# Strassen's scheme moved from the MLPs' first product to their second

## The chip, the cores and the metric

The kernel runs on one core of one Trainium2 chip. A core has five engines with a queue each, in order: TensorE (PE in the profile; its weight loads are PEld), VectorE (DVE), ScalarE (ACT), GpSimd (POOL) and SyncE (SP, which issues the DMAs here). TensorE writes its sums into PSUM, eight banks of 128 x 512 float32; everything else lives in SBUF. The metric is the device time of one execution in microseconds, the median of several runs.

## The reference

A decoder trunk of two layers over 512 tokens of width 1024, in float32. Layer 0 mixes by two kinds of sparse attention, layer 1 by differential attention; each layer adds its mixer's output projection to the residual stream h and then the MLP, and a last norm follows.

```python
def sq_relu_mlp(h, w_up, w_down):
    u = jnp.einsum('btd,df->btf', h, w_up)
    return jnp.einsum('btf,fd->btd', jnp.square(jax.nn.relu(u)), w_down)

x = x + mixer(rms_norm(x, mix_norm_g[i]))
x = x + sq_relu_mlp(rms_norm(x, mlp_norm_g[i]), w_up[i], w_down[i])
```

`w_up` is 1024 x 4096, `w_down` 4096 x 1024, per layer.

## The kernel before

**Precision.** Every float32 product is made from three matmuls (`mm3`, L607): an operand is split into a high part, a copy rounded to the type `F32R`, made on ACT, and a low part, the rest, made by a subtraction on VectorE. high x high, high x low and low x high are added up in PSUM. A weight tile of 128 x 1024 therefore costs a DMA, a cast (L501) and a subtraction (L278, the helper `sub`, or L504).

**Order of the work.** The program is written as Python generators that a planner (`Sched`) runs while the kernel is built: each `op` names its engine, an estimated cost and a priority (a smaller number goes first), and the planner lays down each engine's instructions in the order that its model gives. On the chip each engine then runs its queue in that order. Where the planner sees TensorE idle, it lays down filler matmuls of zeros (L372, `junk`) that keep its clock up. Buffers are `Slots`: PSUM banks, 12 tiles `x4s` of SBUF, two raw weight tiles, weight tiles in pairs (high, low), two pairs outside the MLPs and four within (`Weights.run`, L449). Weights are loaded, cast and subtracted in the order of `plan` (L563), ahead of use as far as the slots reach; the first `w_up` loads of each layer are an exception, spawned at the start and waiting for the MLP's pool alone (`load_up`, L480).

**MLP** (`mlp`, L853). The 4096 hidden columns go in four groups of 1024; each group makes its part of u and adds its part of u² `w_down` to h. The first product uses the Strassen-Winograd scheme, seven products of half-sized blocks for eight: a group has two blocks of 512 hidden columns, and each block takes seven products (`product`, L874) of 24 matmuls of 256 columns, each product in half a pair of blocks. The four sums of the weights are made on VectorE (`split_up`, L514, tiles `ws`), the four sums of x once per layer (`Mixed.quarter`, L740, tiles `ts` and `xm`), and the products are put together on VectorE in SBUF (`sums`, L921: seven adds of 512 columns per block). The squared ReLU follows in `finish` (L910). The second product is plain (`gemm_tok`, L774, tag `down`): two halves of 512 output columns, 96 matmuls of 512 columns each, then `residual` (L808) adds the four banks to h and multiplies by the square of the norm's factor r, so that x needs no r before.

**Around it.** `out_proj` (L1983) runs in two passes over four column blocks; as each block of the second pass is added to h, a `quarter` of the MLP's x is made from it. At the end of layer 0, `follow` (L834) makes the eight chunks of layer 1's x (`Norm.chunk`, L629: four transposes on TensorE, a scaled copy on ACT, a subtraction on VectorE), the first four after the left half of h is whole, the last four after the right one. `odd` (L1773), layer 1's mixer, is started by `trunk` (L2094) when `block` of layer 0 has returned. It makes `qk` and `v` of four pairs of heads by `gemm_tok`, and one pass of `qk` holds four PSUM banks until it is evacuated with the factor r. `finish` (L2063) is the last norm: per row tile, POOL multiplies the left half of h by the gains once its sum of squares is there, then ACT scales the left and VectorE the right half.

Of the kernel before, what the change touches and what calls it, by code (L numbers as in the profile page):

```python
# [19 lines left out]
NT, ND = 4, 8  # L20
# [245 lines left out]
def trunk_kernel(ctx, tc, x, mix_g, mlp_g, w_in0, pe, cw1, cw2, w_out0, w_in1, lam, sub_g, w_out1,  # L266
# [148 lines left out]
    class Weights:  # L415


        def __init__(self):
            self.specs, self.ready = [], {}
            self.raw, self.w = Slots(sch, range(2)), Slots(sch, range(4))  # L420
            self.braw, self.st, self.pool = Slots(sch, range(2)), Slots(sch, range(3)), None
# [10 lines left out]
        def up(self, W, f0, layer):  # L432
            self.add("up", [W[k * 512:k * 512 + 512, f0:f0 + 512].rearrange("(k p) n -> p k n", p=128)
                            for k in range(2)], [128, 4, 512], layer)
# [4 lines left out]
        def move(self, a, b, n):  # L439

            for _ in range(n):
                i = yield a.get(prio=9)
                if i < 4:
                    b.put(i)
# [4 lines left out]
        def run(self):  # L449
            w, phase = self.w, None  # L450
            for i, spec in enumerate(self.specs):
                if spec[0] == "up" and self.specs[i - 1][3] is None:
                    spawn(self.load_up(i, None))
            for i, (tag, srcs, shape, layer, ready) in enumerate(self.specs):
                if layer != phase:
                    if layer is None:
                        spawn(self.move(w, self.w, 4 + 4))
                        w = self.w
                    else:
                        w = yield ev("wp", layer)  # L460
                        spawn(self.move(self.w, w, 4))
                    phase, n = layer, 0
                size = shape[1] * shape[2]
                if tag == "up":
                    n += 1
                    if n > 1:
                        spawn(self.load_up(i, w))
                    yield ready
                    continue
                r = yield self.raw.get()  # L470
                raw = wpool.tile(shape, F32, name="wraw", tag=f"wraw{r}")
# [5 lines left out]
                spawn(self.split(i, shape, raw, r, self.load(i, size, load), w, w.get(2), ready,  # L477
                                 i > 0 and layer is None))

        def load_up(self, i, w):  # L480
            tag, srcs, shape, layer, ready = self.specs[i]
            first = w is None
            if first:
                self.pool = yield ev("mp", layer)
                w = Slots(sch, range(4, 4 + 4))
                sch.set(ev("wp", layer), w)
            ids, futs = [w.get(2) for _ in UP], {m: Fut() for m in UP}
            rs, raws, fs = [], [], []
            for src in srcs:
                rs.append((yield self.braw.get()))  # L490
                raws.append(self.pool.tile(shape, F32, name="braw", tag=f"br{rs[-1]}"))
                fs.append(self.load(i, shape[1] * shape[2], lambda r=raws[-1], src=src: nc.sync.dma_start(r, src)))
            spawn(self.split_up(futs, raws, rs, fs, w, ids, None if first else False))
            sch.set(ready, futs)
# [14 lines left out]
        def split(self, i, shape, raw, r, loaded, w, ids, ready, both):  # L509
            yield loaded  # L510
            yield from self.halves(raw, shape, ids, w, ready, both)
            self.raw.put(r)

        def split_up(self, futs, raws, rs, loaded, w, ids, both):  # L514

            shape = [128, 4, 256]
            ids = dict(zip(UP, ids))
            (a11, a21), (a12, a22) = [[r[:, :, i * 256:i * 256 + 256] for i in range(2)] for r in raws]

            def part(m, src):  # L520
                return spawn(self.halves(src, shape, ids[m], w, futs[m], both))

            def total(x, y, o):
                k = yield self.st.get()
                s = self.pool.tile(shape, F32, name="ws", tag=f"ws{k}")
                yield sub(s, x, y, 1024, 1, o, both is None)
                return k, s

            yield loaded[0]
            f11 = part("a11", a11)  # L530
            yield loaded[1]
            f12 = part("a12", a12)
            k1, s1 = yield from total(a21, a22, OP.add)
            k2, s2 = yield from total(s1, a11, OP.subtract)
            f2 = part("s2", s2)
            k3, s3 = yield from total(a11, a21, OP.subtract)
            f3, f1 = part("s3", s3), part("s1", s1)

            def release(fs, slots, k):
                yield fs  # L540
                slots.put(k)

            spawn(release([f11], self.braw, rs[0]))
            spawn(release([f3], self.st, k3))
            spawn(release([f1], self.st, k1))
            k4, s4 = yield from total(a12, s2, OP.subtract)
            f4, f22 = part("s4", s4), part("a22", a22)
            spawn(release([f2], self.st, k2))
            spawn(release([f12, f22], self.braw, rs[1]))
# [1603 lines left out]
```

## Time and profile before

| | us |
|---|---|
| median of 3 runs (1280.49 to 1281.98) | 1281.44 |
| the profiled execution | 1279.79 |
| its span, first to last instruction | 1278.0 |
| VectorE busy | 919.4 |
| TensorE filler (L372, 266 matmuls) | 34.1 |
| mixer and projection of layer 0, to the first product of its MLP | 321.6 |
| MLP of layer 0, to its last matmul | 662.2 |
| mixer and projection of layer 1, to the first product of its MLP | 905.4 |
| MLP of layer 1, to its last matmul | 1268.6 |

A matmul's duration in the profile overlaps the next one's, so rates are read from starts. The filler counts as busy time of TensorE. A group's row ends with the idle time of the engine before these instructions and what ended it.

### The profile page before, as it was taken

How to read it: one execution, taken by the hardware profiler on the slowest of the kernel's cores; microseconds unless marked ns; L12 is line 12 of the kernel's file. 1: busy time of each engine (PE TensorE's matmuls, PEld its weight loads, DVE VectorE, ACT ScalarE, POOL GpSimd, SP SyncE). 2: the span in 40 equal slices, each digit the busy share in tenths (PEclk: the TensorE clock that was granted, in tenths of full speed). 3: DMA queues.
4: the chain of work that ended last, by engine and by line, in shares of the span. 5: the costliest groups of instructions: out<-in, count | busy, mean ns of one | idle time of the engine just before them, and what ended most of it. 6: DMA issues, size and time to landing. Idle time of an engine off the chain costs nothing.

```text
span 1278.0 us, 21371 instructions
## 1 busy us (share of the span) xinstructions
PE 1260.2 (99%) x8595; PEld 1114.1 (87%) x8595; DVE 919.4 (72%) x1466; ACT 577.0 (45%) x1149; POOL 269.4 (21%) x335
## 2 busy tenths in 40 slices
PE   9999999999999999999999999999999999999998
PEld 7998776779998989989888888889898898998987
DVE  4689986667975965948745687777697586594873
ACT  5556565554642422414334565564454242241332
POOL 1475785443100000000002335333110000000001
PEclk9999999999999999999999999999999999999999
DMA  6212422003232242231322222240423215223131
GB/s 191 73 45 76 116 85 66 18 17 109 91 112 87 80 151 95 75 129 67 115 89 96 65 67 67 66 133 30 153 67 99 100 67 165 80 86 132 67 99 66
DMA packets 78787, 114.70 MB, mean 90 GB/s; under 512 B 4288, under 2 KB 43616, under 8 KB 78688
## 3 DMA queue, kind: packets, MB, share of 16 engines
q1 hardware_dynamic: 78512, 113.27, 27.7%
q8 instruction: 67, 1.10, 0.4%
q14 instruction: 32, 0.26, 0.1%
q10 hardware_dynamic: 176, 0.07, 0.0%
HBM read 109.13 MB, written 4.19 MB: 89 GB/s over the span
## 4 chain that ended last, share of the span: by engine, by line
PE 86%; DVE 7%; ACT 2%; DMA 2%; issue 1%; POOL 1%; SPq 0%; POOLq 0%; DVEq 0%; ACTq 0%
PE b L608 24%; PE b L610 23%; PE b L609 23%; PE b L1076 4%; PE b L1615 2%; PE b L1602 2%; DMA braw<-in_mlp_w_up_dram 2%; PE b L1081 1%; PE b L372 1%; PE b L1037 1%; DVE ts L279 1%; PE b L1413 1%; DVE xm L279 1%; PE b L1900 1%; DVE ws L278 1%
## 5 line engine op out<-in xcount | busy, mean ns | idle before, releaser
L609 PE MATMUL b<-xm,w 128*128 128x256 f32 x896 | 253.9, 283 | 1.3 <-DVE xm L279 1.3
L610 PE MATMUL b<-xm,w 128*128 128x256 f32 x896 | 253.9, 283 | 0.8 <-DVE w L278 0.8
L608 PE MATMUL b<-xm,w 128*128 128x256 f32 x896 | 254.1, 284 | 0.3 <-ACT xm L716 0.3
L608 PE MATMUL b<-w,x 128*128 128x256 f32 (+3 forms) x768 | 243.7, 317 | 0.2 <-ACT eo L1860 0.2
L501 ACT CAST w<-wraw 128x1024 fp32r<-128x1024 f32 (+3 forms) x136 | 137.3, 1010 | 218.7 <-PE b L610 169.3
L609 PE MATMUL b<-w,x 128*128 128x256 f32 (+3 forms) x768 | 234.5, 305 | 0.3 <-DVE w L504 0.3
L610 PE MATMUL b<-w,x 128*128 128x256 f32 (+3 forms) x768 | 234.1, 305 | 0.0
L608 PE MATMUL b<-w,u 128*128 128x512 f32 x512 | 199.4, 389 | 0.0
L609 PE MATMUL b<-w,u 128*128 128x512 f32 x512 | 199.3, 389 | 0.0
L610 PE MATMUL b<-w,u 128*128 128x512 f32 x512 | 199.2, 389 | 0.0
L609 PEld LDWEIGHTS b<-xm,w 128*128 128x128 f32 x896 | 172.0, 192 | 2.1 <-DVE xm L279 1.7
L610 PEld LDWEIGHTS b<-xm,w 128*128 128x128 f32 x896 | 172.0, 192 | 1.4 <-DVE w L278 1.4
L608 PEld LDWEIGHTS b<-xm,w 128*128 128x128 f32 x896 | 172.0, 192 | 1.1 <-ACT xm L716 0.8
L608 PEld LDWEIGHTS b<-w,x 128*128 128x128 f32 x768 | 146.6, 191 | 10.1 <-issue 3.5
L609 PEld LDWEIGHTS b<-w,x 128*128 128x128 f32 x768 | 146.8, 191 | 5.8 <-DVE w L504 0.5
L610 PEld LDWEIGHTS b<-w,x 128*128 128x128 f32 x768 | 146.4, 191 | 5.7
L278 DVE TENSOR_TENSOR w<-wraw,w 128x1024 fp32r<-128x1024 f32 (+1 forms) x65 | 80.1, 1232 | 64.0 <-ACT w L501 64.0
L1021 POOL TENSOR_TENSOR raw<-raw,tm 128x512 f32<-128x512 f32 (+1 forms) x26 | 36.4, 1404 | 403.2 <-DVE raw L1018 381.5
L501 ACT CAST w<-ws 128x1024 fp32r<-128x1024 f32 x64 | 66.4, 1049 | 119.3 <-PE b L610 57.6
L610 PEld LDWEIGHTS b<-w,u 128*128 128x128 f32 x512 | 96.1, 188 | 20.0
L608 PEld LDWEIGHTS b<-w,u 128*128 128x128 f32 x512 | 96.1, 188 | 19.8
L609 PEld LDWEIGHTS b<-w,u 128*128 128x128 f32 x512 | 96.1, 188 | 19.6
(250 smaller groups left out, 2074.9 us busy)
## 6 DMA issues: line engine op xcount, KB each, us to landing
braw<-in_mlp_w_up_dram SPq DMA_DIRECT2D x32, 1024.0 KB, 6.7
wraw<-in_mlp_w_down_dram SPq DMA_DIRECT2D x64, 512.0 KB, 3.9
wraw<-in_odd_w_in_dram SPq DMA_DIRECT2D x32, 256.0 KB, 3.0
wraw<-in_even_w_in_dram SPq DMA_DIRECT2D x12, 512.0 KB, 3.7
wraw<-in_even_cmp_w_dram SPq DMA_DIRECT2D x16, 256.0 KB, 3.8
wraw<-in_even_w_out_dram SPq DMA_DIRECT2D x8, 512.0 KB, 4.4
wraw<-in_odd_w_in_dram SPq DMA_DIRECT2D x8, 512.0 KB, 3.5
q<-in_x_dram SPq DMA_DIRECT2D x4, 512.0 KB, 6.9
```

What stands on the lines that cost most here:

```text
L278: return op("dve", cv(n), lambda: nc.vector.tensor_tensor(o, x, y, op=alu), prio=prio, port=True)
L279: return op(DP, (cv(n), cg(n)), lambda e: e.tensor_tensor(o, x, y, op=alu), prio=prio, bias=0)
L372: nc.tensor.matmul(still[i][:, :256], z[:, :128], z[:, :256], start=True, stop=True)
L501: yield op("act", cas(size), lambda: nc.scalar.copy(wh, src), prio=1)
L608: nc.tensor.matmul(o, ah, bh, start=start, stop=False)
L609: nc.tensor.matmul(o, ah, bl, start=False, stop=False)
L610: nc.tensor.matmul(o, al, bh, start=False, stop=stop)
L1021: yield op("pool", cg(n), lambda: nc.gpsimd.tensor_tensor(o, v, t2, op=OP.add), prio=4)
L1037: nc.tensor.transpose(ps[:, tsl(j)], src, ident)
L1076: nc.tensor.matmul(s[:, j, :n], qs[j][a][half], k[h][b][half, :n], start=i + j == 0, stop=mask is None and i == 2)
L1602: nc.tensor.transpose(ps[:, tsl(k)], p_(a)[:, tsl(kb)], ident)
L1615: nc.tensor.matmul(po.columns(half)[64 * b:64 * b + 64], v1, pt[:, 256 * b:256 * b + 256], start=first, stop=last)
```

## The change

The first product becomes plain: per group four strips (`up`) of 256 hidden columns, each 48 matmuls of 512 columns in two banks, over an x that is kept whole in the MLP's pool (`Kept` in the place of `Mixed`). The factor r is now applied with the ReLU in `hidden`, from a tile `rows` that holds r along the free dimension in all partitions; `spread` makes it with a matmul of ones and a diagonal of r.

The second product takes the scheme, with tokens and output columns halved: u's forms (`a11`, `a12`, `s1` to `s4`, `a22`) are made per strip in `hidden`, the forms of `w_down` (`b11`, `b21`, `t1` to `t4`, `b22`) in `quarters`. Its seven products of 24 wide matmuls are accumulated in banks that are not cleared in between, and each bank's state is added to a quarter of h (`add`) when it stands for one. All 4096 hidden columns' weights are loaded once, as before, in 512 KB tiles; there are eight raw tiles within an MLP, and `w_up` has no path of its own in `Weights.run`.

The `odd` mixer is started at once; its products begin as soon as the chunks they read are there, and only their evacuation waits for the end of layer 0. They take the right half of x first (`ODD_ORDER`).

```diff
+    DOWN = ("b11", "b21", "t2", "t1", "t3", "b22", "t4")
+    ODD_ORDER = (2, 3, 0, 1)
...
+        def quarters(self, j, loaded, futs, ids, w, raws):
+            shape = [128, 2, 512]
...
+            b11 = yield from fetch("b11")
+            f11 = part("b11", b11)
+            b21 = yield from fetch("b21")
+            f21 = part("b21", b21)
+            b12 = yield from fetch("b12")
+            yield f11
+            yield sub(b11, b12, b11, 1024, 1)
+            b22 = yield from fetch("b22")
+            k = yield self.st.get()
+            t2 = self.pool.tile(shape, F32, name="ws", tag=f"ws{k}")
+            yield sub(t2, b22, b11, 1024, 1)
+            f2 = part("t2", t2)
+            spawn(release(part("t1", b11), "b11"))
+            yield sub(b12, b22, b12, 1024, 1)
+            spawn(release(part("t3", b12), "b12"))
+            spawn(release(part("b22", b22), "b22"))
+            yield f21
+            yield sub(b21, b21, t2, 1024, 1)
+            spawn(release(part("t4", b21), "b21"))
+            yield f2
+            self.st.put(k)
...
+        def spread(self):
+            yield ev(self.name, "r", 0, NT)
+            def a():
+                for t in range(NT):
+                    nc.vector.tensor_scalar(self.diag[:, tsl(t)], ident, self.r[:, t:t + 1], None, op0=OP.mult)
+            yield op("dve", 4 * cv(64), a, prio=1, port=True)
+            b = yield banks.get(prio=1)
+            ps = bank(b)
+            yield op("pe", 0.87, lambda: nc.tensor.matmul(ps, ones.bitcast(F32), self.diag, start=True, stop=True), prio=1)
+            yield op("act", ca(T), lambda: nc.scalar.copy(self.rows, ps), prio=1)
...
+            def prio(m, i):
+                k = ("a11", "a12", "s2", "s1", "s3", "s4", "a22").index(m)
+                return 2 if i >= 2 and k >= LATE else k - 9
+            def parts(g, i, m, src):
+                hi, lo = yield from form(g, m)
+                yield op("act", cas(256), lambda: nc.scalar.copy(hi[:, i], src), prio=prio(m, i))
+                yield sub(lo[:, i], src, hi[:, i].bitcast(F32), 256, prio(m, i))
+            def hidden(g, i, ids, ps):
...
+                def out(n):
+                    yield op("dve", cv(T) + 0.06, lambda: nc.vector.scalar_tensor_tensor(
+                        v[:, n], ps[n], 0.0, norm.rows, op0=OP.max, op1=OP.mult), prio=-1)
+                    banks.put(ids[n])
+                    yield op("act", cas(T), lambda: nc.scalar.activation(v[:, n], v[:, n], AF.Square), prio=-1)
...
+            def up(g, i):
+                ids = yield banks.get(2, prio=-1)
...
+                            for n in range(2):
+                                mm3(ps[n], wh[:, c, tsl(n)], wl[:, c, tsl(n)], norm.x(0, 4 * kb + c),
+                                    norm.x(1, 4 * kb + c), kb == 0 and c == 0, kb == 1 and c == 3)
+                        yield op("pe", 6 * cm(512), run, prio=9)
...
+                spawn(hidden(g, i, ids, ps))
+            def add(g, j, l, ps, last):
+                def one(n):
+                    t = 2 * j + n
+                    hs = h["t"][:, t, l * 512:l * 512 + 512]
+                    yield ev("h", h["name"], l)
+                    yield op("dve", cv(T), lambda: nc.vector.tensor_tensor(hs, ps[n], hs, op=OP.add), prio=1)
...
+            def down(g):
+                ia, a = yield from two()
+                ib, b = yield from two()
...
+                for k, (m, ps) in enumerate((("a11", a), ("a12", b))):
+                    yield from step(g, m, ps, True, 3, late[k])
...
+                    if k == 0:
+                        f = add(g, 0, 0, a, False)
...
+                spawn(free(add(g, 0, 0, b, True), ib))
+                yield f
+                yield from product(g, "s2", a, False)
+                f = add(g, 0, 1, a, False)
+                ic, c = yield from two()
+                yield from product(g, "s1", c, True)
+                fc = add(g, 1, 1, c, False)
+                yield f
+                yield from product(g, "s3", a, False)
+                f = add(g, 1, 1, a, True)
+                yield fc
+                yield from product(g, "s4", c, False)
+                spawn(free(add(g, 0, 1, c, True), ic))
+                yield f
+                yield from product(g, "a22", a, False)
+                spawn(free(add(g, 1, 0, a, True), ia))
             for g in range(4):
...
+                for i in range(4):
+                    yield from up(g, i)
+                yield from down(g)
...
     def trunk():
-        yield from block(0, spawn(even(outs[0])), ev("even"), outs[0], x_src, n2)
-        yield from block(1, spawn(odd(n2, outs[1])), ev("oddp"), outs[1], spill, Norm("nf", None, None))
+        mixers = [spawn(even(outs[0])), spawn(odd(n2, outs[1]))]
+        yield from block(0, mixers[0], ev("even"), outs[0], x_src, n2)
+        fire("odd")
+        yield from block(1, mixers[1], ev("oddp"), outs[1], spill, Norm("nf", None, None))
```

`product` now goes through two weight tiles, two steps of six matmuls on each; `step` waits for the strip's part of the form.

More of the change, by code (lines that the diff above doesn't have):

```diff
@@ L475, in load @@
                         nc.sync.dma_start(dst(raw), src)
-                spawn(self.split(i, shape, raw, r, self.load(i, size, load), w, w.get(2), ready,
+                spawn(self.split(i, shape, raw, r, self.load(i, size, load), w, raws, w.get(2), ready,
                                  i > 0 and layer is None))
[L480 to L494, printed above, removed]
         def halves(self, src, shape, ids, w, fut, both=True):
@@ L507, in halves, with split @@
             sch.set(fut, (wh, wl, lambda: w.put(*ids)))
-        def split(self, i, shape, raw, r, loaded, w, ids, ready, both):
+        def split(self, i, shape, raw, r, loaded, w, raws, ids, ready, both):
             yield loaded
             yield from self.halves(raw, shape, ids, w, ready, both)
[L512 to L518, printed above, removed]
-            def part(m, src):
[L521 to L549, printed above, removed]
-            spawn(release([f4], self.st, k4))
@@ L635, in chunk @@
                 yield ev(self.name, "xt", c // 2)
+        def chunk(self, c, prio=2):
+            yield from self.take(c)
             b = yield banks.get()
@@ new lines, in mlp, with form @@
+            uv, us = Slots(sch, range(2)), Slots(sch, range(2))
+            norm.open(mp)
+            forms, LATE = {}, 3
+            def prio(m, i):
+                k = ("a11", "a12", "s2", "s1", "s3", "s4", "a22").index(m)
+                return 2 if i >= 2 and k >= LATE else k - 9
+            def form(g, m):
+                if (g, m) not in forms:
+                    forms[g, m] = None
+                    ids = (12, 13) if m == "a11" else (yield x4s.get(2))
+                    if m == "a11" and g:
+                        yield ev(layer, "a11", g - 1)
+                    pool = mp if m == "a11" else xpool
+                    forms[g, m] = (ids, [pool.tile([128, 4, 256], F32R, name="u", tag=f"x{i}") for i in ids])
+                    fire(layer, "form", g, m)
+                yield ev(layer, "form", g, m)
+                return forms[g, m][1]
@@ new lines, in product, with step, run @@
+            def product(g, m, ps, first):
+                for j in range(2):
+                    w = yield wq.get("down")
+                    yield from step(g, m, ps, first, 2 * j, w)
+                    yield from step(g, m, ps, first, 2 * j + 1, w)
+                    w[2]()
+                done(g, m)
+            def step(g, m, ps, first, i, w):
+                yield ev(layer, "u", g, m, i)
+                hi, lo = forms[g, m][1]
+                def run():
+                    for n in range(2):
+                        mm3(ps[n], hi[:, i, tsl(n)], lo[:, i, tsl(n)], w[0][:, i % 2], w[1][:, i % 2],
+                            first and i == 0, i == 3, not first)
+                yield op("pe", 6 * cm(512), run, prio=9)
```

459 lines of the change are left out of this document (186 added, 273 removed).

## The prediction

> **What bounds the kernel now.** I read the page's busy shares and its chain first.
>
> ```profile
> PE 1260.2 (99%) x8595; PEld 1114.1 (87%) x8595; DVE 919.4 (72%) x1466; ACT 577.0 (45%) x1149; POOL 269.4 (21%) x335
> PE 86%; DVE 7%; ACT 2%; DMA 2%; issue 1%; POOL 1%; SPq 0%; POOLq 0%; DVEq 0%; ACTq 0%
> ```
>
> TensorE is busy for 99% and carries 86% of the chain; VectorE has 7%. So time can go in two ways: less TensorE work, or less waiting at the few places where VectorE stands in the chain. "Busy" hides the second kind, because line 372 fills waits with matmuls of zeros that no result uses.
>
> Next I need the rate of each kind of matmul. In layer 0 the second group of the MLP (all rows here: start, duration) goes:
>
> ```profile
> 408.84 0.28 PE L608 MATMUL b<-xm,w 128*128 128x256 f32 x1
> ...
> 449.16 0.40 PE L608 MATMUL b<-w,u 128*128 128x512 f32 x1
> ...
> 492.70 0.28 PE L608 MATMUL b<-xm,w 128*128 128x256 f32 x1
> ```
>
> and the groups of instructions in those two stretches are, for one of the three lines of `mm3` in each,
>
> ```profile
> L608 PE MATMUL b<-xm,w 128*128 128x256 f32 x112 | 31.7, 283 | 0.0
> ```
> ```profile
> L608 PE MATMUL b<-w,u 128*128 128x512 f32 x64 | 24.9, 389 | 0.0
> ```
>
> The durations (283 and 389 ns) overlap, so I take starts: 336 narrow matmuls (256 columns) in 40.32 us are 0.1200 us each, 192 wide ones (512 columns) in 43.54 us are 0.2268 each. Two narrow ones do the work of one wide one and cost 0.0132 us more. Nothing waits in here.
>
> The waits are elsewhere. The view by stretches (length, then busy time and count for PE, PEld, DVE, ACT, POOL) for the start of the MLP in layer 0, the border between the layers, and the start of the MLP in layer 1:
>
> ```profile
> 301.90:365.20 63.30, 62.19 (x519) 61.33 (x519) 59.61 (x76) 36.36 (x61) 15.45 (x7) 1.00 0.19 60
> 662.20:667.50 5.30, 5.02 (x45) 4.47 (x45) 4.49 (x12) 4.57 (x11) 0.00 (x0) 1.00 0.28 90
> 895.20:973.40 78.20, 74.24 (x609) 71.22 (x608) 67.56 (x89) 39.28 (x64) 11.34 (x5) 1.00 0.30 100
> ```
>
> Of these counts, the groups give as filler (L372) and as transposes (L726, L641), for the three stretches in turn:
>
> ```profile
> L726 PE MATMUL b<-cst,h 128*128 128x128 f32 x32 | 4.4, 274 | 1.0 <-DVE h L2006 1.0
> L372 PE MATMUL b<-still 128*128 128x256 bf16 x17 | 2.0, 273 | 0.0
> ```
> ```profile
> L372 PE MATMUL b<-still 128*128 128x256 bf16 x28 | 3.4, 273 | 0.0
> L641 PE MATMUL b<-cst,h 128*128 128x128 f32 x16 | 2.1, 276 | 0.3 <-DVE h L821 0.3
> ```
> ```profile
> L372 PE MATMUL b<-still 128*128 128x256 bf16 x73 | 8.8, 273 | 0.0
> L726 PE MATMUL b<-cst,h 128*128 128x128 f32 x32 | 4.6, 278 | 1.2 <-DVE h L2006 1.2
> ```
>
> Eight transposes take 0.79 us of TensorE:
>
> ```profile
> 301.96 1.04 PE L726 MATMUL b<-cst,h 128*128 128x128 f32 x8
> 302.75 0.36 PE L608 MATMUL b<-w,x 128*128 128x256 f32 x1
> ```
>
> Layer 0: 519 − 32 − 17 = 470 narrow matmuls x 0.12 = 56.4, transposes 3.2, so **3.7 us** of the 63.3 are waiting. Layer 1: 609 − 32 − 73 = 504 x 0.12 = 60.5, and 3.2: **14.5 us** of 78.2. The border: 1.6 us of transposes and 0.1 of a matmul's end, so **3.6 us** of 5.3. What the chain shows in layer 1's start:
>
> ```profile
> 896.89 9.52 DMA braw<-in_mlp_w_up_dram
> ...
> 911.27 1.13 DVE ts L279
> ...
> 928.12 2.83 DVE ts L279
> ```
>
> These are the 1 MB weight loads, which stand ahead of the output projection's own weights on SP, and VectorE's sums (`ts`) for a Strassen scheme on the first product.
>
> **The change, part by part.** *The products.* The first one becomes plain: 4 strips x 48 = 192 wide matmuls a group. The second gets the scheme: 7 x 24 = 168 wide ones. The multiplied columns stay the same (336 x 256 + 192 x 512 = 360 x 512), but all matmuls are wide: 360 x 0.2268 = 81.65 us for 83.86. That is 2.21 us in each of eight groups: **−17.7**. The form (128x128 stationary, 128x512 moving) is in the trace; only that banks alternate every three matmuls is new.
>
> The Trainium skill, "TensorE: Matmul & The Clock Gate", section "Back-to-back issue gap", gives a warm gap of N/2.4 + 2.5 ns. By it 1344 instructions fewer would save an estimated 3.4 us instead; the two rows disagree (13.2 ns, not 2.5), and the same forms return here, so I stay with the rows, and keep the rule's outcome as a rival.
>
> *Starts of the MLPs.* The sums of x go; x is transposed, scaled and split, as `Norm.chunk` does. After the projection's last column block only chunks 6 and 7 are late; six steps of the first strip (six matmuls each, 1.36 us) can run before them, 8.2 us, while an add, transpose, copy and subtraction take about 0.7 + 0.8 + 0.7 + 0.7 (rows for each stand here or below). The first `w_up` tiles now come in order behind the projection's weights, in 512 KB loads; the nearest load (1 KB rows too) and cast are
>
> ```profile
> L501 ACT CAST w<-ws 128x1024 fp32r<-128x1024 f32 x64 | 66.4, 1049 | 119.3 <-PE b L610 57.6 <-DVE ws L278 38.7 <-PE b L609 12.2
> wraw<-in_even_w_out_dram SPq DMA_DIRECT2D x8, 512.0 KB, 4.4
> ```
>
> and 4.4 + 1.05 (cast) + 1.22 (subtraction) = 6.7 us fit into the last two column blocks (2 x 5.8 us) if the buffers allow it. I leave 1.5 us of waiting in layer 0 and 2 in layer 1, about the 1.0 to 1.2 us that L726 still waits for an add, and a bit; bounds nothing and all of it. **−2.2 and −12.5.** Added: a row of norm factors is spread by a matmul in plain float32, as the chain shows two of,
>
> ```profile
> 885.26 0.86 PE b L1945 x2
> ```
>
> so 0.43 each in two passes, 0.86 per layer: **+1.7**. Its chain (squares, root, spread) must end before the eight banks are full, four strips or 43 us later, so only TensorE's own time counts.
>
> *The border.* The scheme ends the right half of h first, and the first `qk` tiles need that half (`ODD_ORDER`). While `a22` runs (24 x 0.2268 = 5.4 us) chunks 4 to 7 can be made; the `qk` products on them (48 wide ones, 10.9 us) cover chunks 0 to 3. The evacuation waits until the pools have changed, but four banks hold a whole `qk` pass of 21.8 us. The weights' loads and the spill keep their order on SP. I leave 0.5: **−3.1**. The `qk` steps have the better priority; if they overtake `a22`, its add and the left chunks are late instead and up to 3.6 returns.
>
> *New waits.* Within a group's second product one add is poorly covered: `a` is added to h after `a11`, before `s2` goes on in it, and only the last step of `a12` lies between. VectorE begins 0.43 us after a last matmul's start, an add takes 0.68, and TensorE follows 0.05 after it:
>
> ```profile
> 1268.37 0.39 PE L610 MATMUL b<-w,u 128*128 128x512 f32 x1
> 1268.80 0.75 DVE L821 SCALAR_TENSOR_TENSOR h<-b,r,h 128x512 f32<-128x512 f32 x1
> ...
> 1273.53 0.75 DVE L2088 SCALAR_TENSOR_TENSOR h<-h,fin,gb 128x512 f32<-128x512 f32 x1
> ```
> ```profile
> 309.26 0.68 DVE L2006 TENSOR_TENSOR h<-b,part 128x512 f32<-128x512 f32 x1
> 309.99 0.88 PE L726 MATMUL b<-cst,h 128*128 128x128 f32 x6 [1.03 <-DVE h L2006]
> ```
>
> 1.16 us, against 0.23 + 1.36 = 1.59 of cover. A weight subtraction just begun on VectorE (1.22) makes it up to 0.8 late; queued behind the waiting matmul is all of TensorE. I take 0.25 x 8 = **+2.0**, between 0 and 6.4. The other adds have a whole product (5.4 us) over them.
>
> *VectorE, the cover of all this.* Groups in the two halves of a group before, and one form of 256:
>
> ```profile
> 408.80:449.10 40.30, 40.30 (x337) 40.26 (x337) 35.60 (x42) 17.64 (x21) 0.00 (x0) 1.00 0.21 68
> 449.10:492.60 43.50, 43.50 (x194) 36.03 (x194) 23.66 (x27) 10.61 (x12) 0.00 (x0) 1.00 0.41 132
> ```
> ```profile
> L278 DVE TENSOR_TENSOR w<-ws,w 128x1024 fp32r<-128x1024 f32 x7 | 8.5, 1219 | 2.3 <-ACT w L501 2.3
> ```
> ```profile
> L1048 DVE TENSOR_TENSOR qk<-b,qk 128x256 fp32r<-128x256 f32 x32 | 12.3, 415 | 4.0 <-ACT qk L1047 4.0
> ```
>
> After, a group needs 8 + 14 weight subtractions and 8 sums at 1.22 (36.6), four strips of 2 x 0.75 and 11 x 0.415 (24.3), 14 adds at 0.68 (9.5): 70.4 us of 81.65, 86%, where 59.3 of 83.8 was needed. Before, the first half stood at 88% and TensorE had no gap, with the same four pairs of weight tiles at 24 x 0.12 = 2.88 us each; the new second product uses one in 12 x 0.2268 = 2.72. So I cost it at nothing, with little to spare.
>
> *The end.* Now the left half of the last two row tiles comes last, and POOL multiplies it (two at 1.54 us):
>
> ```profile
> L655 ACT ACTIVATE junk<-h 128x512 bf16<-128x512 f32 x32 | 20.1, 629 | 25.3 <-DVE h L821 23.9 <-DVE fin L2071 0.6 <-DVE h L2006 0.5
> L2069 POOL TENSOR_TENSOR h<-h,gb 128x512 f32<-128x512 f32 x4 | 6.0, 1543 | 300.3 <-ACT junk L655 300.3
> ```
>
> From the last matmul's end (0.23 after its start): the add of the first tile is done at about 0.3, its square at 1.0, POOL's two steps follow until about 4.2, and the scaling, a pass of ACT like the square, until 4.9 or 5.3. Before, the last step on VectorE (quoted above, 1273.53) ended 1274.28 − 1268.60 = 5.7 after it. **0**, give or take 1.5.
>
> **The sum.** −17.7 − 2.2 − 12.5 + 1.7 − 3.1 + 2.0 = −31.8. The profiled execution took 1279.8 us (span 1278.0), so 1248.0; the median of the runs lies 1.6 above it, and I say **1249.5**.
>
> **Rivals.** *Slower: VectorE becomes the bound in the second product.* If nothing is made ahead, that stage has 14 subtractions and 8 sums (26.8), 14 adds (9.5), the last strip (6.1) and the late forms of the third (6 x 0.415 = 2.5): 44.9 us under 38.1 of TensorE (168 x 0.2268), 6.8 too much; eight times that, without the +2.0, gives 1249.5 + 52 = 1302. It turns slower than before when 4.0 us a group are lost, so when less than 2.8 of the 44.9 are done early. Against it: half the sums need only loaded tiles and can lie under the first product, which has half the weight steps. 6%.
>
> *The starts keep their waits.* If the first `w_up` tiles, or the norm's row, come only after the projection ends, 6.7 us are waited in each layer, for the 1.5 and 2 allowed above, and the border returns too: 1249.5 + 13.4 − 3.5 + 3.1 = 1262.5. For it: the loads now stand behind the projection's in one order. Against: those tiles leave their buffers a block or more before the end. 16%.
>
> *Wide matmuls save little.* If what a narrow one costs more belongs to something that stays (each switch of banks, now every three matmuls), up to 17.7 returns: at most 1267. Nothing in the stretches above shows a cost at a switch. (By the Trainium skill's rule quoted above it would be 14.3, an estimate of 1264.) 4%.
>
> *The early start does nothing*: `qk` waits or overtakes; then 1252.5, inside the forecast's own spread.
>
> **Chances.** Forecast 72% (1241 to 1257: all waits gone is −38, tail and adds at their bounds +8), starts 16%, narrow 4%, slower 6%, and 2% for a mixture that ends near no change. 1240 to 1264 leaves out about 2 in 10. A measurement can tell about 0.2% from no change: faster 0.91, same 0.03, slower 0.06.
>
> **What would show it.** Only 512-wide matmuls in the MLPs, starts 0.227 us apart, and groups of about 82 us; stretches of filler at the two starts and at the border nearly gone; `qk` matmuls right behind `a22`; waits of PE on the add to h under 0.8 us, once a group. Wrong would be: PE waiting on the weight subtractions within the second product, or filler before the first strip.

## The result and the profile after

| | before | after |
|---|---|---|
| median (lowest to highest), us | 1281.03 (1280.49 to 1281.98) | 1250.06 (1248.51 to 1251.11) |
| profiled execution, us | 1279.79 | 1250.05 |
| its span, us | 1278.0 | 1247.9 |

The ratio is 0.9757, with a 95% interval of 0.974 to 0.9773: 2.4% faster, 0.6 us above the forecast. Line numbers are those of the kernel after: `mm3` is L614 to L616, transposes of x L651, `spread`'s matmul L723, the adds to h L867; L278 (`sub`) and L372 (filler) have kept theirs.

The two rows of the profile's page after the change that answer to those shown of before are the engine totals and the chain:

```profile
PE 1235.1 (99%) x7199; PEld 1037.4 (83%) x7199; DVE 942.5 (76%) x1670; ACT 633.9 (51%) x1338; POOL 248.9 (20%) x326
PE 93%; DVE 3%; ACT 1%; POOL 1%; issue 1%; DMA 1%; SPq 0%; POOLq 0%; ACTq 0%
```

TensorE is at 99% as before, with 1396 matmuls fewer (filler among them), and VectorE's share of the chain has gone from 7% to 3%, although its busy time rose by 23 us: what has gone is waiting for VectorE at particular places. The stretches after the change (length, then busy time and count for PE, PEld, DVE, ACT, POOL, then the granted clock) are: start of the MLP in layer 0, second product and first product of its next group, border of the layers, start of the MLP in layer 1:

```profile
302.50:366.30 63.80, 63.80 (x360) 55.70 (x360) 47.51 (x82) 33.92 (x66) 0.00 (x0) 1.00 0.38 123
366.30:405.40 39.10, 39.10 (x178) 32.20 (x178) 32.77 (x44) 17.93 (x23) 0.00 (x0) 1.00 0.44 134
405.40:448.90 43.50, 43.50 (x194) 36.02 (x193) 31.49 (x54) 18.57 (x36) 0.00 (x0) 1.00 0.25 74
649.30:654.80 5.50, 5.50 (x34) 4.76 (x34) 3.17 (x5) 3.27 (x8) 1.98 (x1) 1.00 0.29 95
883.50:952.00 68.50, 68.50 (x400) 60.37 (x399) 51.20 (x88) 36.30 (x73) 1.80 (x1) 1.00 0.45 147
```

In both starts PE's busy time now equals the length; the groups show no filler in that of layer 0 and three matmuls of it in that of layer 1. One group starts on TensorE as follows (first matmul of the second product, of the next first product, of the next second one):

```profile
366.35 0.39 PE L614 MATMUL b<-w,u 128*128 128x512 f32 x1
...
405.37 0.39 PE L614 MATMUL b<-xm,w 128*128 128x512 f32 x1
...
448.89 0.39 PE L614 MATMUL b<-w,u 128*128 128x512 f32 x1
```

The first product takes 43.52 us, 192 x 0.2267, as worked out. The second takes 39.02 where 168 matmuls make 38.10, and a group 82.54 where the prediction had 81.65. The 0.89 us between are one wait, the same in all eight groups. This is the timeline of VectorE and of TensorE's L614 and filler around one of them:

```profile
960.08 1.23 DVE L278 TENSOR_TENSOR w<-ws,w 128x1024 fp32r<-128x1024 f32 x1
...
961.22 1.22 DVE L278 TENSOR_TENSOR wraw<-wraw,ws 128x1024 f32<-128x1024 f32 x1
...
962.35 1.28 DVE L867 TENSOR_TENSOR h<-b,h 128x512 f32<-128x512 f32 x2
962.87 1.05 PE L372 MATMUL b<-still 128*128 128x256 bf16 x8
...
963.67 0.48 PE L614 MATMUL b<-w,u 128*128 128x512 f32 x1
```

The two adds after `a11`, one for each bank, end at 963.63, and `s2` starts 0.04 us later. Eight filler matmuls (0.80 us) stand between `a12` and `s2`; since the second add ends as late as they do, the wait is real and not only the planner's. The last step of `a12`, six matmuls of 0.2268, began at 961.51; `a11` ended six matmuls before, and the first bank was done three matmuls earlier still, so by the prediction's 0.43 us the first add could have begun at about 961.03. VectorE was in a subtraction until 961.2, and then a sum for `t4` stood ahead of the adds for another 1.13 us.

The border of the layers, on TensorE:

```profile
650.27 1.91 PE L651 MATMUL b<-cst,h 128*128 128x128 f32 x16
651.93 0.48 PE L614 MATMUL b<-w,u 128*128 128x512 f32 x1
...
654.77 0.39 PE L614 MATMUL b<-w,x 128*128 128x512 f32 x1
...
657.49 1.91 PE L651 MATMUL b<-cst,h 128*128 128x128 f32 x16
659.16 0.48 PE L614 MATMUL b<-w,x 128*128 128x512 f32 x1
```

Four chunks are transposed within `a22`, `qk` follows on it at 654.77, and the other four chunks stand after twelve of the `qk` matmuls. There is no filler in this stretch.

**Where the 30.1 us of the span went.** The two starts are read from the first transposes (layer 0: 301.96 before, 302.55 after) or from the projection's second pass (layer 1: 895.29 and 883.75) to the second product (365.30 and 366.35, 973.47 and 951.99). Layer 0's took 63.34 us and takes 63.80; layer 1's took 78.18 and takes 68.24. Less the 3.2 that the plain first product adds in each, and less 0.86 for `spread`, their waits fell by 3.6 and 14.0; some 0.4 and 0.5 are left.

| part | us |
|---|---|
| matmuls | −17.7 |
| waits at the start of layer 0 | −3.6 |
| waits at the start of layer 1 | −14.0 |
| the border | −3.6 |
| `spread` | +1.7 |
| the wait before `s2` (8 x 0.89) | +7.1 |
| the end | −0.1 |
| layer 0's mixer up to its first transposes | +0.6 |
| layer 1's mixer, from the first `qk` matmul to the projection's second pass, transposes aside | −0.5 |
| sum | −30.1 |

### The profile page after: what moved, and what is told of

It is laid out like the page before. It is cut to its first block, busy times and chain, and to the rows that moved or that the text cites. A ratio compares the mean times of both kernels' runs of the same rounds, so it can differ in the third digit from the quotient of the medians.

```text
span 1247.9 us, 19052 instructions
## 1 busy us (share of the span) xinstructions
PE 1235.1 (99%) x7199; PEld 1037.4 (83%) x7199; DVE 942.5 (76%) x1670; ACT 633.9 (51%) x1338; POOL 248.9 (20%) x326
## 4 chain that ended last, share of the span: by engine, by line
PE 93%; DVE 3%; ACT 1%; POOL 1%; issue 1%; DMA 1%; SPq 0%; POOLq 0%; ACTq 0%
PE b L614 26%; PE b L616 26%; PE b L615 25%; PE b L1043 4%; PE b L1582 2%; PE b L1569 2%; PE b L372 2%; PE b L1048 1%; PE b L1004 1%; PE b L651 1%; PE b L1380 1%; PE b L1886 1%; DMA q<-in_x_dram 1%; DVE sc L1354 0%; PE b L1612 0%
## 5 line engine op out<-in xcount | busy, mean ns | idle before, releaser
L504 ACT CAST w<-wraw 128x1024 fp32r<-128x1024 f32 (+3 forms) x232 | 238.7, 1029 | 358.7 <-PE b L616 193.5
L278 DVE TENSOR_TENSOR w<-wraw,w 128x1024 fp32r<-128x1024 f32 (+1 forms) x161 | 197.1, 1224 | 97.2 <-ACT w L504 96.5
L614 PE MATMUL b<-w,x 128*128 128x256 f32 (+3 forms) x768 | 243.6, 317 | 0.2 <-ACT eo L1846 0.2
L616 PE MATMUL b<-w,x 128*128 128x256 f32 (+3 forms) x768 | 234.3, 305 | 0.0
L614 PE MATMUL b<-xm,w 128*128 128x512 f32 x512 | 200.2, 391 | 0.0
L615 PE MATMUL b<-xm,w 128*128 128x512 f32 x512 | 199.2, 389 | 0.0
L616 PE MATMUL b<-xm,w 128*128 128x512 f32 x512 | 199.2, 389 | 0.0
L614 PE MATMUL b<-w,u 128*128 128x512 f32 x448 | 175.2, 391 | 0.0
L616 PE MATMUL b<-w,u 128*128 128x512 f32 x448 | 174.4, 389 | 0.0
L615 PE MATMUL b<-w,u 128*128 128x512 f32 x448 | 174.3, 389 | 0.0
L614 PEld LDWEIGHTS b<-w,x 128*128 128x128 f32 x768 | 146.7, 191 | 10.1 <-issue 3.5
L616 PEld LDWEIGHTS b<-w,x 128*128 128x128 f32 x768 | 146.5, 191 | 5.7
L507 POOL TENSOR_TENSOR w<-wraw,w 128x1024 fp32r<-128x1024 f32 (+3 forms) x26 | 58.4, 2248 | 424.3 <-ACT w L504 423.8
L615 PEld LDWEIGHTS b<-xm,w 128*128 128x128 f32 x512 | 96.1, 188 | 20.3 <-issue 0.5
L614 PEld LDWEIGHTS b<-xm,w 128*128 128x128 f32 x512 | 96.1, 188 | 20.1 <-issue 0.5
L616 PEld LDWEIGHTS b<-xm,w 128*128 128x128 f32 x512 | 96.1, 188 | 20.0
L616 PEld LDWEIGHTS b<-w,u 128*128 128x128 f32 x448 | 84.1, 188 | 17.6
L615 PEld LDWEIGHTS b<-w,u 128*128 128x128 f32 x448 | 84.1, 188 | 17.4
L614 PEld LDWEIGHTS b<-w,u 128*128 128x128 f32 x448 | 84.1, 188 | 17.2
L507 DVE TENSOR_TENSOR w<-wraw,w 128x1024 fp32r<-128x1024 f32 (+2 forms) x45 | 55.4, 1230 | 28.6 <-ACT w L504 27.3
```

The lines of the kernel that those rows point to most:

```text
L278: return op("dve", cv(n), lambda: nc.vector.tensor_tensor(o, x, y, op=alu), prio=prio, port=True)
L504: yield op("act", cas(size), lambda: nc.scalar.copy(wh, src), prio=1)
L507: lambda e: e.tensor_tensor(wl, src, wh.bitcast(F32), op=OP.subtract), prio=1)
L614: nc.tensor.matmul(o, ah, bh, start=start, stop=False, skip_group_check=more)
L615: nc.tensor.matmul(o, ah, bl, start=False, stop=False, skip_group_check=more)
L616: nc.tensor.matmul(o, al, bh, start=False, stop=stop, skip_group_check=more)
```

## The experiments

The ratio of each kernel is to the kernel before, run beside it on the same chip; that one had medians from 1281.0 to 1282.3. The first four runs below and the sixth start from the kernel after.

**1. More cover for the first add.** The last step of `a11` goes ahead of the last two of `a12`:

```diff
-                for k, (m, ps) in enumerate((("a11", a), ("a12", b))):
-                    yield from step(g, m, ps, True, 3, late[k])
...
+                for k, i in ((0, 0), (0, 1), (0, 2), (1, 0), (1, 1), (0, 3), (1, 2), (1, 3)):
```

> The last step of a11 is put before the last two steps of a12, so the add of a11 to h has 2.72 us of TensorE work over it and not 1.36. Theory 1: the one stretch of filler per group (0.80 us, eight of them) is the wait for this add, which stands behind a 1.22 us weight sum on VectorE; with the longer cover it goes, and 8 x 0.88 = 7.0 us with it: 1243. Theory 2: VectorE as a whole is short in the second product; then the wait only moves, and the time stays at 1250 within 1.5.

The result is 1242.29 us (1242.11 to 1242.72), ratio 0.9693 [0.9679, 0.9706]. The first matmuls of the same second product and of the next one:

```profile
366.51 0.39 PE L614 MATMUL b<-w,u 128*128 128x512 f32 x1
...
448.11 0.39 PE L614 MATMUL b<-w,u 128*128 128x512 f32 x1
```

A group takes 81.60 us, with no filler in the second product. The span is 7.3 us shorter than after the change (1240.6 for 1247.9): the wait was worth what the eight gaps add up to, and nothing took its place.

**2. The add first in VectorE's queue.** Here the order on TensorE stays, and the planner prefers the adds to the weights' work:

```diff
-                    yield op("dve", cv(T), lambda: nc.vector.tensor_tensor(hs, ps[n], hs, op=OP.add), prio=1)
+                    yield op("dve", cv(T), lambda: nc.vector.tensor_tensor(hs, ps[n], hs, op=OP.add), prio=-10)
```

> All adds to h go ahead of everything else on VectorE (priority -10 for 1); the steps of TensorE keep their places. If the wait before s2 is the add's place behind a weight sum that could as well come later, the filler goes and the time falls by 6 to 7 us: 1243 to 1244. If the add is not yet ready when VectorE takes up that sum, the order can't help: 1250 within 1. If VectorE as a whole is short, the sums that now come later are waited for instead: 1250 or more.

The result is 1242.37 us (1241.92 to 1243.47), ratio 0.9694 [0.968, 0.9708]: the same gain, and again no filler in the second product. So what made the add late was its place in the queue; the sum that gave way was not missed later. Either edit makes a kernel about 3.1% faster than the one before.

**3. Without the early start.** The products of `odd` wait for the end of layer 0 again:

```diff
+            yield ev("odd")
```

> The first qk product waits until layer 0 has ended, as before the change; all else is that of after. Theory 1: the border's wait returns, 3.6 us as before, and up to 1 more since the left half of h now ends last: 1253.5 to 1255. Theory 2: the early start is worth nothing, since the evacuation of qk waits for the end of layer 0 in either case: 1250 within 1.

The result is 1252.9 us (1252.02 to 1254.53), ratio 0.9774 [0.9759, 0.9788], 2.2 (by the ratios) to 2.8 us (by the medians) more than with it. The border on TensorE:

```profile
655.68 0.94 PE L372 MATMUL b<-still 128*128 128x256 bf16 x7
656.45 1.91 PE L651 MATMUL b<-cst,h 128*128 128x128 f32 x16
658.20 3.00 PE L372 MATMUL b<-still 128*128 128x256 bf16 x26
660.96 0.48 PE L614 MATMUL b<-w,x 128*128 128x512 f32 x1
```

Filler of 0.77 and 2.76 us (start to start) is back: 3.5 us, the border's wait of before. The profiled spans are 4.5 apart, more than the medians, because the profiled execution is the slowest of the five: another 0.9 was lost before the border (the first transposes in `a22` start at 651.18, for 650.27), in layer 0's mixer, which the edit doesn't touch. There the granted clock stood at 0.50 for 3.41 us from 99.5 on in this profile, and at 1.00 in the profile after.

**4. Narrow matmuls in the first product.** Each 512-wide matmul is cut into two of 256, all else as it is:

```diff
+                                for q in (slice(0, 256), slice(256, 512)):
+                                    mm3(ps[n][:, q], wh[:, c, tsl(n)], wl[:, c, tsl(n)], norm.x(0, 4 * kb + c, q),
```

> In the first product each wide matmul is cut into two of 256 columns: 1536 instructions more, the same multiplied columns. Theory 1 (the rows of before, 0.1200 and 0.2268 us from start to start): 1536 x 0.0132 = 20.3 us longer, 1270. Theory 2 (2.5 ns a matmul, the Trainium skill's gap in TensorE: Matmul & The Clock Gate, section Back-to-back issue gap): an estimate of 3.8 us longer, 1254.

The result is 1265.26 us (1264.6 to 1265.96), ratio 0.987 [0.9854, 0.9887], 15.2 us more. A first product of the narrow kind, and the second one behind it:

```profile
405.73 0.28 PE L614 MATMUL b<-xm,w 128*128 128x256 f32 x1
...
451.81 0.40 PE L614 MATMUL b<-w,u 128*128 128x512 f32 x1
...
490.34 0.28 PE L614 MATMUL b<-xm,w 128*128 128x256 f32 x1
```

The first product takes 46.08 us = 384 x 0.1200, for 43.52: 2.56 us a group, 20.5 in eight. About 4 of it came back at the wait before `s2`, whose filler fell from 0.80 to 0.31 us, presumably since VectorE got more time. Another 1.6 us (the first product starts at 319.40, for 321.02) do not belong to the edit, which leaves layer 0's mixer as it is; most of them come from a granted clock of 0.50, which the profile after has there for 3.41 us from 159.9 on and this one has not. So cutting a matmul in two costs 13.3 ns (2.56 us / 192) at the same number of columns, close to the 13.2 that the two rates of the kernel before give. The Trainium skill, "TensorE: Matmul & The Clock Gate", section "Back-to-back issue gap", gives 2.5 ns a matmul beside its columns, which would make this run an estimated 3.8 us longer; the measurement decides.

**5. The order of the loads.** On the kernel before: the first up loads of each layer in their turn, behind the projection's weights.

```diff
-            for i, spec in enumerate(self.specs):
-                if spec[0] == "up" and self.specs[i - 1][3] is None:
-                    spawn(self.load_up(i, None))
...
+                        spawn(self.load_up(i, None))
```

> The kernel before, with the first w_up loads of each layer issued in their turn behind the output projection's weights, and not ahead of them. Theory 1: the wait of 14.5 us at the start of layer 1's MLP comes from these loads, on SP ahead of the projection's own (9.5 us in the chain); without that about 5 remain: 1281 - 9.5 = 1271.5. Theory 2: it comes from VectorE's sums for the scheme on x; then the time stays at 1281 within 2, or grows, since the first w_up tiles come later.

The result is 1282.09 us, ratio 1.0006 [0.9996, 1.0016]: no change. In the profiled execution layer 1's start takes 78.1 us (78.2 before), with the granted clock at 0.50 for 3.41 us of it, and layer 0's takes 65.9 (63.3). So moving the loads on SP, whose place the prediction read from the chain as a part of layer 1's wait, gives none of that wait back, and costs some in layer 0. Runs 7 to 12 start from the kernel before, too.

**6. Twice the low parts of `w_down`.** Each is subtracted twice over, 14 more subtractions a group:

```diff
+                if both is False and shape[2] == 512:
+                    yield sub(wl, src, wh.bitcast(F32), size, 1, both=both is None)
```

> In the second product each low part of a weight tile is computed twice, 14 subtractions of 128 x 1024 more per group on VectorE; nothing else changes. Theory 1 (what counts is VectorE's start to start, 1.14 us for such a subtraction): 62.6 + 16.0 = 78.6 us a group under 82.5, so there is room and the time grows by less than 10: 1250 to 1260. Theory 2 (its durations count, 1.22): 70.4 + 17.1 = 87.5, 5 us too much in each of eight groups: 1290. Theory 3 (the second product alone counts, nothing can be made ahead): 38.1 us of TensorE under 35 + 16 = 51 of VectorE, 1350 or so.

The result is 1334.8 us (1334.44 to 1335.16), ratio 1.0412 [1.0393, 1.0431], 85 us more than the kernel after: between the second theory and the third. The second product's stretch of one group:

```profile
365.90:416.30 50.40, 47.66 (x241) 37.44 (x239) 47.88 (x62) 18.62 (x26) 0.00 (x0) 1.00 0.34 101
```

VectorE is busy for 95% of it, and the stretch is 11.4 us longer for about 16 us of added work (14 x 1.14). Over the whole group there would have been 82.5 − 64.3 = 18.2 us to spare (the two stretches after sum to 32.77 + 31.49 = 64.3), but the work for this product was not done under the first one; that four pairs of weight tiles don't let it be far ahead is the likely reason, which no run tested. The margin is that of the stage: 32.8 of 39.1 us, 84%.

**7 and 8. What made the start of layer 1 wait.** Two parts of VectorE's work are left out of the kernel before, one at a time: the sums of x, and the sums of the weights.

```diff
-            def total(m, x, y):
-                yield sub(self.ts[m][:, s], x, y, 512, -1, both=1)
...
-                yield from total("t1", right, left)
...
-                fs += [spawn(self.parts("t1", self.ts["t1"][:, s], j))]
+                fs += [spawn(self.parts("t1", right, j))]
```

> The kernel before with one thing left out of each layer: the eight subtractions (128x512, 0.68 us each on VectorE) that make the sums t1 to t4 of x; the first product's forms are cast and subtracted from x's own blocks in their place, so the first product computes something else than u. The number of matmuls, casts and low parts stays. At stake is what held up the start of layer 1's MLP (14.5 us of waits in the kernel before, 3.7 in layer 0), now that the order of the weight loads was shown not to. Theory A, the sums of x on VectorE: each stands in the chain from the add to h to the first product that uses the form, so at least half of the 14.5 goes: 1281 minus 7 or more, 1274 or less. Theory B, the sums of the weights and their low parts in front of that chain on VectorE: at most 2 us go, 1279 to 1281. Theory C, the length of the chain itself (add, transposes, scaled copy, cast, low part): at most 2 us here too, and nothing by the next run either.

```diff
-            k1, s1 = yield from total(a21, a22, OP.add)
-            k2, s2 = yield from total(s1, a11, OP.subtract)
-            f2 = part("s2", s2)
+            f2 = part("s2", a22)
```

> The kernel before without the four sums of each block's up weights (128x1024, 1.22 us each on VectorE, 8 blocks a layer): the forms are cast and subtracted from the raw blocks in their place, so again the first product computes something else than u. x's sums stay. Theory A: no more than 2 us, 1279 to 1281. Theory B: VectorE is rid of about 4 x 1.22 = 4.9 us of work in layer 1's start, and most of the 14.5 us goes with it: 1274 or less. Theory C: nothing, 1280 to 1282. In the groups after the first the first product had no gap on TensorE, so no theory expects a gain there.

Without x's sums 1275.19 us (1272.73 to 1276.51), ratio 0.9939 [0.9923, 0.9956]; without the weights' 1270.44 (1269.73 to 1271.43), 0.9909 [0.9894, 0.9924]. Run 7 lies between the outcomes of its theories A and B, run 8 has that of B. The stretch from the projection's second pass to the second product, in layer 1, is shown first before, then without x's sums, then without the weights':

```profile
895.00:973.50 78.50, 74.54 (x612) 71.47 (x611) 67.67 (x89) 39.43 (x65) 11.34 (x5) 1.00 0.30 100
```
```profile
893.30:969.80 76.50, 72.63 (x586) 70.22 (x586) 62.91 (x82) 38.61 (x66) 8.87 (x4) 0.96 0.29 98
```
```profile
892.70:963.70 71.00, 68.30 (x567) 66.85 (x566) 61.68 (x87) 39.59 (x67) 10.17 (x5) 1.00 0.33 108
```

The work of TensorE in it is 60.5 + 3.2 = 63.7 us, as in the prediction. The weights' sums were worth 7.5 us of the wait, x's 2.0, under a granted clock of 0.96 (and each 2 us in layer 0). The prediction's chain had shown `ts`, the sums of x.

**9. Neither sum.**

> Both of the last two edits on the kernel before: neither the sums of x (eight of 0.68 us a layer) nor those of the weights (four of 1.22 us a block) are made, the products run on x's and the weights' own blocks. The stretch from the start of the projection's second pass in layer 1 to the first matmul of the second product took 78.4 us before, 14.5 of it waits; 76.4 without x's sums (with the granted clock at 0.6 to 0.7 for a while) and 71.0 without the weights'. If the two sums on VectorE are the whole cause and add up: 64 to 66 us, and the time 1263 to 1267. If a good part is the chain's own length (add, transposes, copy, cast, low part), which stays: 68 us or more, 1268 or more. If they stand for each other (VectorE is free as soon as one is gone): about 71, 1270.

The result is 1270.73 us (1269.28 to 1273.08), ratio 0.9915 [0.9896, 0.9933]: no more than without the weights' sums alone. The gains don't add up, and 8.3 us of waits stay in 72.0. What the first product waits for here, on ScalarE and TensorE (in brackets the idle time ahead and what ended it):

```profile
902.18 1.04 ACT L501 CAST w<-braw 128x1024 fp32r<-128x1024 f32 x1 [5.64 <-DMA braw<-in_mlp_w_up_dram]
...
903.13 1.14 ACT L701 CAST xm<-xf 128x512 fp32r<-128x512 f32 x2
...
903.79 0.38 PE L593 MATMUL b<-xm,w 128*128 128x256 f32 x1 [1.29 <-ACT xm L701]
...
905.14 0.38 PE L594 MATMUL b<-xm,w 128*128 128x256 f32 x1 [0.96 <-DVE xm L279]
```

The cast of x, whose input was there from 899.2 on, stands in ScalarE's queue behind the cast of a 1 MB up tile that has not landed. And the granted clock (the eighth column, behind POOL) falls after it, in stretches of 5 us:

```profile
900.00:905.00 5.00, 2.89 (x22) 2.49 (x21) 1.75 (x3) 2.33 (x4) 0.00 (x0) 1.00 0.79 289
905.00:910.00 5.00, 4.57 (x25) 4.17 (x26) 4.59 (x7) 4.94 (x12) 2.14 (x1) 0.66 0.05 15
910.00:915.00 5.00, 5.00 (x44) 5.00 (x43) 2.94 (x5) 1.92 (x5) 0.00 (x0) 1.00 0.31 98
```

Over the whole stretch the clock was 0.98 here and 0.96 in run 7, which makes an estimated 72 x 0.02 = 1.4 and 76.5 x 0.04 = 3.1 us of it. So x's sums alone may be worth up to 5 us, and on top of the weights' sums still under half a microsecond (72.0 − 1.4 for 71.0).

**10 and 11. One of the up tiles loaded early**, into a tile outside the MLP's pool, without the weights' sums and without both:

```diff
+            if first and layer == 1:
+                yield ev("mp", 0)
+                for k, src in enumerate(srcs[:1]):
...
+                    raws.append(wpool.tile(shape, F32, name="braw", tag=f"bx{k}"))
```

> The kernel before without the sums of the weights, as two runs ago, and besides the first 1 MB up tile of layer 1 has a raw tile of its own outside the MLP's pool and is loaded during layer 0's MLP (the room comes from the sums' tiles). In the run without any sums the chip showed ScalarE idle for 5.64 us until that load was there (902.18), the cast of x queued behind the cast of the weights, and TensorE behind both. Moving the loads later had changed nothing, but they can't come later than they did without harm; earlier is the other half of that test. If the late load is part of layer 1's wait: the first products start without the idle 1 to 1.2 us each, the stretch from the projection's second pass to the second product falls from 71.0 to 67 to 69.5, the time from 1270.4 to 1267 to 1269. If it isn't: 70.5 to 71.5 and 1270 to 1271.

> The same early load with neither sum made. Without it this stretch took 72.0 us, with the granted clock at 0.66 from 905 to 910 after the idle time at 902 to 905. If the late load and the clock's dip behind it are what hid the gain of leaving out x's sums: the dip goes, the stretch falls to 65 to 68 and the time to 1264 to 1267. If the chain's own length keeps it: 69 or more, 1268 or more.

The results are 1270.49 and 1270.4 us, ratios 0.9924 [0.9902, 0.9946] and 0.9917 [0.9897, 0.9937]: nothing. The stretches take 70.1 and 72.0 us, for 71.0 and 72.0 without the early load. The early tile was cast as soon as the pool opened, but the second 1 MB tile, which found no room outside, was the next in ScalarE's queue, ahead of the cast of x. It landed only 0.6 and 0.8 us before the first tile of runs 8 and 9 (900.09 for 900.69, 901.32 for 902.08). In run 10 ScalarE still waited for it:

```profile
900.11 1.05 ACT L508 CAST w<-braw 128x1024 fp32r<-128x1024 f32 x1 [3.99 <-DMA braw<-in_mlp_w_up_dram]
```

This settles nothing on the loads; it shows only that half of them is not enough.

**12. Run 8 with the loads in the order of run 5.**

> The kernel before with the first up loads in their turn behind the projection's weights (which alone changed nothing) and without the sums of the weights (which alone took the stretch from the projection's second pass to the second product from 78.4 to 71.0 us). The question is whether the loads' order was hidden behind VectorE's sums. If so, it pays once they are gone: 69.5 us or less, 1269 or less, and less waiting at the projection's third and fourth blocks. If the order has no part in layer 1's wait at all: 70 to 72 us and 1269.5 to 1272, or more in layer 0, where the late loads cost some 3 us before.

The result is 1269.07 us (1268.74 to 1270.69), ratio 0.9906 [0.989, 0.9923]; the stretch takes 70.9 us (71.0 in run 8). On TensorE:

```profile
923.38 0.87 PE L709 MATMUL b<-cst,h 128*128 128x128 f32 x6 [2.30 <-DVE h L1989]
924.09 2.89 PE L372 MATMUL b<-still 128*128 128x256 bf16 x25
```

Now the projection's blocks run without a gap until 916.38, and the waiting stands behind them. The order of the loads decides where TensorE waits in this stretch, not how long. Of the 14.5 us, 7.5 thus go with the weights' sums, x's sums share in the same ones, and some 7 were taken away by none of these runs. The change took those as well. What else it has (512 KB tiles, eight raw tiles, strips that need one weight tile at a time) was not tried alone, and which of these does it stays open.

## Why the prediction was right

*The products*: −17.7 came out as worked out from starts; run 4 confirms 13.3 ns for each matmul more. It has twice the matmuls at the same number of switches between banks, so with it the rival of a switch cost falls.

*Starts of the MLPs*: the mechanism was right in that the waits went with the first product's scheme, and the size was short, −3.6 and −14.0 for −2.2 and −12.5, as some 0.4 and 0.5 us were left where 1.5 and 2 were allowed. Its reading of the cause failed in layer 1: the chain's rows named the loads and the sums of x, while runs 5, 7, 8 and 12 give the largest known part to the sums of the weights, and nothing to the loads' order; about half of the wait has no cause that a run shows. The chain names only the last link of each wait.

*`spread`*: +1.7 held. From its start at 328.75 to the next full-rate start at 329.84 it is 1.09 us; less one matmul's 0.23 this makes 0.86 per layer:

```profile
328.75 1.02 PE L723 MATMUL b<-diag,ones 128*128 128x512 f32 x2
329.21 0.80 PE L614 MATMUL b<-xm,w 128*128 128x512 f32 x1
329.84 0.40 PE L615 MATMUL b<-xm,w 128*128 128x512 f32 x1
```

*The border*: −3.6 for −3.1; the trace of run 3 gives 3.5 of it to the early start, its times 2.2 to 2.8. The rival that it does nothing falls.

*The wait before `s2`* is the term that was mis-sized: +7.1 for +2.0, beyond its bound of 6.4. Right were the place, the product and who is queued behind it. Wrong was the size. The value was a mean over chances (0.25 of 0.8), while the order is laid down once: all eight groups had the same wait, and all of the bound, 0.80 us of filler. The 0.09 beyond the bound is the first matmul behind the filler, 0.48 us long for 0.39, which the prediction did not count. That the bound itself came out is partly luck: it let one weight subtraction, just begun, stand ahead of one add; there were the rest of one and a whole one more, put there by the planner's order, and then two adds. Runs 1 and 2 took the wait away.

*VectorE at nothing* held: run 6 shows how much it takes. But the estimate it was weighed by, 70.4 us a group, was high (64.3), for durations overlap: in the timeline of the wait two L278 of 1.23 and 1.22 us are followed by the next start after 1.14 and 1.13. The margin that counts was the second product's 84%. *The end* changed by −0.1, within its 1.5.

That the time came out 0.6 us from the forecast is luck, for the errors nearly cancel: starts and border were 3.4 us better than forecast, the wait 5.1 worse, and the rest adds up to nothing (the end −0.1, the two mixers +0.6 and −0.5). So the span fell by 30.1 for the sum's 31.8, and the profiled execution by 29.7. Of the 2.05 us by which that one misses the 1248.0, the median shows only 0.6, as it now agrees with the profiled execution, where the prediction had added 1.6. The nearness says less than the terms do.

## What to carry to other kernels

In an order that is laid down when the kernel is built, a thin cover can fail in every round alike, as it did in all eight here. Look up which instructions stand ahead of the one that is waited for, and charge the wait to every round. The cure is a step of other work between, or a better place in the queue, and it was worth 7 us here. When a whole start of a stage waits, the last link that the chain names need not be the one to remove: leave each suspect out and see what the stage gives back. And before two profiles are compared, look for stretches at half clock: here one of 3.41 us put most of 1.6 us between the profiles of run 4 and of the kernel after, in code that was the same.

## What the hardware showed unexpectedly

In run 9 TensorE stood idle for 1.29 and 0.96 us in close succession without filler, and the granted clock was 0.66 in the 5 us that followed. In run 7 it waited for 0.90, 0.96 and 1.84 us between 903.4 and 909.1, and the clock was 0.71 and 0.61 from 905 to 915. But a single idle time of 1.94 us in run 10, and one of 2.30 us in run 12, quoted above, left it at 1.00.

In these runs the clock follows how the idle time falls into fixed stretches. In all fourteen profiles the granted clock changes only at whole multiples of 3.41 us after it first reached 1.00, and it is 1.00 or 0.50. Cut at these points, two stretches each of runs 9, 10 and 12 are

```profile
902.36:905.77 3.41, 1.16 (x8) 0.82 (x7) 2.52 (x4) 2.92 (x5) 0.00 (x0) 1.00 0.45 150
905.77:909.18 3.41, 3.12 (x15) 2.72 (x15) 3.33 (x4) 3.35 (x10) 2.14 (x1) 0.50 0.01 2
```
```profile
900.24:903.65 3.41, 1.97 (x17) 1.77 (x15) 2.46 (x2) 3.00 (x5) 1.27 (x1) 1.00 0.11 35
903.65:907.06 3.41, 2.91 (x23) 2.67 (x24) 3.41 (x6) 1.48 (x5) 0.00 (x0) 1.00 0.25 79
```
```profile
919.13:922.54 3.41, 1.95 (x17) 1.71 (x15) 3.41 (x4) 2.58 (x5) 1.71 (x2) 1.00 0.00 0
922.54:925.96 3.42, 2.58 (x24) 2.38 (x25) 3.12 (x5) 3.42 (x8) 0.00 (x0) 1.00 0.00 0
```

By PE's busy time, both waits of run 9 fall into one stretch, 2.25 us idle of 3.41, and 0.50 is granted in the next. The wait of run 10 is split into 1.44 and 0.50, and run 12 has 1.46 and 0.84. Over all fourteen profiles, leaving out the last 8 us of each, an idle sum of 1.84 us or more in a stretch was followed by 0.50 every time and one of 1.57 or less never; nine sums from 1.58 to 1.73 went both ways. So the same waits can cost half the clock for 3.41 us in one execution and nothing in another: near 98 us of layer 0's mixer, the same code in run 3 and in the kernel after, the sums were 1.99 and 1.33.

The Trainium skill, "TensorE: Matmul & The Clock Gate", section "What's actually happening", puts the fall behind an idle window of about 3.4 us; here a stretch of 3.41 us with 2.25 idle was enough. Where filler covered waits of this size, in the start of layer 1 in the kernel before, the row shows 1.00.
